# Convolution's input product: ten channel blocks with one product over both halves of x, and VectorE's order of taps and gates written out

## The chip, the cores and the metric

The kernel runs on one core of a Trainium2 chip. The metric is the time of one execution on the device in microseconds (us), the median of several runs. The engines are named as the profile names them: PE (matrix products), PEld (its weight loads), DVE (VectorE), ACT (ScalarE), POOL (GpSimd) and SP (which issues the weights' transfers).

## The reference

A decoder trunk of four residual layers over 256 tokens of 2048 channels, in float32: a convolution module, an MLP, a state-space layer, an MLP, and a last norm. The change lies in the convolution module, the first layer:

```python
def conv_module(h, w_in, b_in, dw, dw_b, ln_g, ln_b, w_out, b_out):
    u = h @ w_in + b_in                       # 256 x 2048 times 2048 x 4096
    a, gate = jnp.split(u, 2, axis=-1)
    v = a * jax.nn.sigmoid(gate)
    v = lax.conv_general_dilated(v, dw[:, None, :], ..., padding=[(30, 0)],
                                 feature_group_count=2048) + dw_b   # 31 taps per channel
    v = layer_norm(v, ln_g, ln_b)
    v = jax.nn.silu(v)
    return v @ w_out + b_out
```

## The kernel before, in words

**Products in float32.** Every operand is split into a high part (rounded to the fast matrix format) and a low part (what is left). A product is high x high + low x high + high x low. Activations lie as hT: channel blocks of 128 on the partitions, and for each block the high and the low part of the 256 tokens side by side (512 columns).

**The stream of weights.** Every layer adds its weights as *steps*; a step is 1 MB and is worked through in two *halves* of 0.5 MB. For each half, ACT converts the raw weights to the high part (L118, `hi`), and DVE or POOL subtracts to get the low part (L125, `lo`). In the convolution's input product the first eight halves have their low part made on DVE, halves 8 to 63 on POOL. There are four buffers each for `hi` and `lo`, so the conversion of a half waits until PE is through with the half four before. SP loads a step when the raw buffer of the step three before is free.

**The input product.** The 16 channel blocks c = 0..15 take four halves each (half h = 4c to 4c+3). Before, every block uses `mm_g`: per half 24 products of 256 columns (high weights with the high half of x, L211; high weights with the low half, L212; low weights with the high half, L213), all into one sum. The MLP's up product uses `mm_f` instead: eight products of 512 columns (high weights with both halves of x at once, L199), then eight of 256 (low weights, L202); the two sums lie side by side in the accumulator and have to be added later (`relu2`, L807 and L808).

**The gate of a block.** When a block's four halves are done, DVE multiplies the accumulator by the norm's factor (L446), ACT takes the sigmoid (L447, `ga`), and DVE combines both into the gated channel block (L448).

**Taps.** For c = 0..11 the depthwise convolution runs on DVE: ACT starts an accumulator (L527, `cv`), and 30 instructions on DVE add a tap each (L829). For c = 12..15 (`PACKED`) it runs on PE as 32 small products per block (L484, `pk`), from four shifted copies R. For 12 to 14 those copies go through DRAM: ACT's queue issues the write (L473, `vd`) and then the four reads (L477). For the last block, DVE and ACT copy them (L468, L470). The small weights for this, `wpk`, are made by ACT (16 small copies `dp`, L379) and POOL (L386). POOL also adds the output bias to x in four pieces (L398, L400).

**Layer norm.** After blocks 0..3 a first sum of their channels is made (L539, `stat`), copied by ACT (L558, `raw`), multiplied out (`mean`), and turned into a shift (L562). The groups 0..3, 4..7 and 8..11 have the shift taken off (L569, one instruction of DVE for four blocks), are squared on ACT (L571) and summed on PE (L539). After the last block the totals are made (`ln_totals`, `ln_finish`) and the output product begins.

**Order.** Each engine works through its own list in order. The lists are made when the program is built: a scheduler places the instructions by its own estimate of times, with `high_priority` for urgent ones, and `behind(x)` makes an instruction stand after x on its engine. The depthwise taps are emitted all 30 at once, so that the scheduler sets where they stand.

## Time and profile before

| | |
|---|---|
| median of 3 runs | 1988.23 us (1988.21 to 1988.59) |
| the profiled execution | 1987.61 us, span 1985.8 us |
| busy in the span | PE 99%, DVE 71%, ACT 48%, POOL 14% |
| granted PE clock | 1.00 in every slice |
| the convolution's input product | about 8 to 214 us of the span |
| PE idle or on small products after it, until the output product is under way | about 214 to 236 us |

The table is read with the profiled execution: it is 0.62 us below the median, and its span leaves out 1.8 us around it. Everything after 236 us is left as it is by the change, and each engine's list there is the same in both kernels.

### The profile page before, as it was taken

What the parts mean: (1) busy time and instruction counts of PE and PEld (TensorE: products, weight loads), DVE (VectorE), ACT (ScalarE), POOL (GpSimd) and SP (SyncE); (2) the same over time, 40 slices, a digit from 0 to 9 for tenths busy, and PEclk for the clock granted to TensorE, in tenths of its full rate; (3) what the DMA queues carried; (4) which work ended last, traced back from release to release, by engine and by line L of the source; (5) the groups of instructions that cost most, each with busy time, mean ns of one, the idle gap of its engine ahead of it and who ended that gap; (6) DMA issues with size and microseconds to landing.
All of it is one profiled execution on the core that took longest, in us unless ns stands there. A gap on an engine that the chain in (4) does not pass through costs nothing.

```text
span 1985.8 us, 28885 instructions
## 1 busy us (share of the span) xinstructions
PE 1966.9 (99%) x11604; PEld 1687.0 (85%) x11604; DVE 1401.3 (71%) x1904; ACT 952.4 (48%) x1179; POOL 274.8 (14%) x252
## 2 busy tenths in 40 slices
PE   8999999999999999999999999999999999999998
PEld 8999788888888888888888788888888888888887
DVE  6899798888787777777558847565555565555655
ACT  6443655544444544444445445454444454444444
POOL 3998300000000221222010000000000000000000
PEclk9999999999999999999999999999999999999999
DMA  8767458667686877877898865665666656565653
GB/s 228 190 184 207 147 183 267 206 226 245 200 260 192 214 229 253 265 246 238 319 308 298 304 215 186 191 191 189 193 190 192 190 191 191 190 213 190 192 191 128
DMA packets 317030, 428.49 MB, mean 216 GB/s; under 512 B 9761, under 2 KB 211553, under 8 KB 313537
## 3 DMA queue, kind: packets, MB, share of 16 engines
q1 hardware_dynamic: 300976, 384.59, 61.6%
q0 software_dynamic: 12352, 37.49, 6.3%
q10 hardware_dynamic: 3568, 4.56, 0.8%
q8 instruction: 91, 1.49, 0.3%
q14 instruction: 43, 0.35, 0.1%
HBM read 400.08 MB, written 34.91 MB: 219 GB/s over the span
## 4 chain that ended last, share of the span: by engine, by line
PE 96%; DVE 2%; DMA 1%; issue 0%; SPq 0%; POOL 0%; ACT 0%; POOLq 0%; DVEq 0%; ACTq 0%
PE acc L199 24%; PE acc L222 15%; PE acc L223 15%; PE acc L224 15%; PE acc L202 12%; PE acc L213 3%; PE acc L212 3%; PE acc L211 3%; PE pk L484 1%; DMA Vt<-Vd 0%; SPq L92 0%; PE kp L1113 0%; PE xw L1254 0%; DMA raw<-in_conv_w_in_dram 0%; PE xt L254 0%
## 5 line engine op out<-in xcount | busy, mean ns | idle before, releaser
L118 ACT ACTIVATE hi<-raw 128x1024 fp32r<-128x1024 f32 x672 | 711.6, 1060 | 953.5 <-PE acc L224 510.2
L125 DVE TENSOR_TENSOR lo<-raw,hi 128x1024 fp32r<-128x1024 f32 x611 | 747.9, 1226 | 505.6 <-ACT hi L118 501.3
L199 PE MATMUL acc<-hT,hi 128*128 128x512 f32 x2048 | 514.4, 393 | 0.0
L199 PEld LDWEIGHTS acc<-hT,hi 128*128 128x128 f32 x2048 | 368.9, 189 | 68.0 <-issue 1.6
L222 PE MATMUL acc<-hi,rT 128*128 128x512 f32 x992 | 387.2, 391 | 0.0
L223 PE MATMUL acc<-lo,rT 128*128 128x512 f32 x992 | 386.4, 390 | 0.0
L224 PE MATMUL acc<-hi,rT 128*128 128x512 f32 x992 | 386.0, 389 | 0.0
L202 PEld LDWEIGHTS acc<-hT,lo 128*128 128x128 f32 x2048 | 279.6, 190 | 20.0
L202 PE MATMUL acc<-hT,lo 128*128 128x256 f32 x2048 | 286.3, 282 | 0.0
L222 PEld LDWEIGHTS acc<-hi,rT 128*128 128x128 f32 x992 | 186.3, 188 | 39.6 <-issue 1.6
L224 PEld LDWEIGHTS acc<-hi,rT 128*128 128x128 f32 x992 | 186.3, 188 | 39.1
L223 PEld LDWEIGHTS acc<-lo,rT 128*128 128x128 f32 x992 | 186.3, 188 | 38.0 <-issue 0.2
L125 POOL TENSOR_TENSOR lo<-raw,hi 128x1024 fp32r<-128x1024 f32 x60 | 143.1, 2402 | 31.3 <-ACT hi L118 24.8
L211 PE MATMUL acc<-hT,hi 128*128 128x256 f32 x512 | 146.1, 286 | 0.9 <-ACT hi L118 0.9
L212 PE MATMUL acc<-hT,hi 128*128 128x256 f32 x512 | 145.7, 286 | 0.3 <-DVE hT L259 0.3
L213 PE MATMUL acc<-hT,lo 128*128 128x256 f32 x512 | 145.5, 286 | 0.0
L829 DVE SCALAR_TENSOR_TENSOR cv<-vT,dw,cv 128x256 f32<-128x256 f32 x348 | 141.3, 486 | 2.2 <-ACT cv L527 1.7
L820 DVE TENSOR_TENSOR x<-x,acc 128x1024 f32<-128x1024 f32 (+1 forms) x72 | 83.6, 1161 | 27.6 <-PE acc L224 22.0
L211 PEld LDWEIGHTS acc<-hT,hi 128*128 128x128 f32 x512 | 98.9, 193 | 3.0 <-issue 1.6
L222 PE MATMUL acc<-hi,yT 128*128 128x512 f32 x256 | 101.1, 395 | 0.0
L212 PEld LDWEIGHTS acc<-hT,hi 128*128 128x128 f32 x512 | 98.8, 193 | 2.2 <-issue 1.6
L223 PE MATMUL acc<-lo,yT 128*128 128x512 f32 x256 | 99.9, 390 | 0.6 <-DVE lo L125 0.6
(285 smaller groups left out, 1722.9 us busy)
## 6 DMA issues: line engine op xcount, KB each, us to landing
raw<-in_mlp_w_up_dram SPq DMA_DIRECT2D x128, 1024.0 KB, 5.8
raw<-in_mlp_w_down_dram SPq DMA_DIRECT2D x128, 1024.0 KB, 5.2
raw<-in_ssm_w_glu_dram SPq DMA_DIRECT2D x32, 1024.0 KB, 5.5
raw<-in_conv_w_in_dram SPq DMA_DIRECT2D x60, 512.0 KB, 5.6
...
```

Of the source, the lines that this page charges most:

```text
L118: self.nc.scalar.activation(hi, sl, AF.Copy)
L125: ins = eng.tensor_tensor(out=lo, in0=sl, in1=hi.bitcast(F32), op=ALU.subtract)
L199: mm(accs[m], lhsT=hi[:, kk, cs[m]], rhs=xT(k0 + kk), start=first and kk == 0, stop=False)
L202: mm(accs[m][:, 0:T], lhsT=lo[:, kk, cs[m]], rhs=xT(k0 + kk)[:, 0, :], start=False, stop=last and kk == 3)
L211: mm(accs[m], lhsT=hi[:, kk, c], rhs=x[:, 0, :], start=first and kk == 0, stop=False)
L212: mm(accs[m], lhsT=hi[:, kk, c], rhs=x[:, 1, :], start=False, stop=False)
L213: mm(accs[m], lhsT=lo[:, kk, c], rhs=x[:, 0, :], start=False, stop=last and kk == 3)
L222: mm(acc[:, b, :], lhsT=ak[:, 0, t], rhs=hi[:, kk, :], start=first and kk == 0, stop=False)
L223: mm(acc[:, b, :], lhsT=ak[:, 0, t], rhs=lo[:, kk, :], start=False, stop=False)
L224: self.mm_last = mm(acc[:, b, :], lhsT=ak[:, 1, t], rhs=hi[:, kk, :], start=False, stop=last and kk == 1)
L820: return self.nc.vector.tensor_tensor(out=out, in0=a, in1=b, op=op)
L829: return self.nc.vector.scalar_tensor_tensor(out=out, in0=a, scalar=s, in1=b, op0=op0, op1=op1)
```

## The change

1. For c = 3..12 (`HALVES`) the block uses `mm_f` in place of `mm_g`. The two sums are added in the gate: ACT copies the second one out of the accumulator (L457 of the changed kernel, `low`), and DVE adds it to the first (L458).
2. DVE's instructions of the stage (adds, multiplies, gates, taps, shifts) stand in one written order (`dve`). Taps are handed out in portions (`taps`): three between a block's multiply and its gate, then 3, 6, 7 and 6 with the next halves, which makes 25 per block, from two chains in turn. `begin_chains` starts an accumulator only when the number of open chains allows it.
3. On ACT, the next conversion of weights stands behind the sigmoid, or behind the `cv` that was started last (`act_first`).
4. In the norm, the group is summed when its last tap is done, the shift stands two halves later, and the centring of a group is emitted at once.

```diff
+HALVES = range(3, 13)
...
-            self.nc.scalar.activation(hi, sl, AF.Copy)
+            with self.behind(self.act_first) if self.act_first is not None else nullcontext():
+                self.nc.scalar.activation(hi, sl, AF.Copy)
+            self.act_first = None
...
-                    self.mm_g([A[:, 0], A[:, 1]], self.hT, hi, lo, kc * 8 + half * 4,
-                              kc == 0 and half == 0, kc == 1 and half == 1)
+                    (self.mm_f if c in HALVES else self.mm_g)([A[:, 0], A[:, 1]], self.hT, hi, lo, kc * 8 + half * 4,
+                                                              kc == 0 and half == 0, kc == 1 and half == 1)
                     if kc == 1 and half == 1:
-                        self.gate(c, A)
+                        self.gate(c, acc)
+                    h = 4 * c + 2 * kc + half
+                    if h >= 6 and not (c == KB - 1 and kc == 1 and half == 1):
+                        self.taps(3 if kc == 1 and half == 1 else 7 if half else 6)
...
-            nc.vector.tensor_tensor(out=A, in0=A, in1=self.rstdB.broadcast_to([P, 2, T]), op=ALU.mult)
-            nc.scalar.activation(t, A[:, 1, :], AF.Sigmoid, bias=b_in[:, KB + c:KB + c + 1])
-            nc.vector.scalar_tensor_tensor(out=self.cblk(c), in0=A[:, 0, :], scalar=b_in[:, c:c + 1], in1=t,
-                                           op0=ALU.add, op1=ALU.mult)
+            if c in HALVES:
+                low = self.t2([P, 2, T], name="low")
+                nc.scalar.activation(low, acc[:, :, T:2 * T], AF.Copy)
+                self.dve(lambda: nc.vector.tensor_tensor(out=A, in0=A, in1=low, op=ALU.add))
+            self.dve(lambda: nc.vector.tensor_tensor(out=A, in0=A, in1=self.rstdB.broadcast_to([P, 2, T]), op=ALU.mult))
+            self.act_first = nc.scalar.activation(t, A[:, 1, :], AF.Sigmoid, bias=b_in[:, KB + c:KB + c + 1])
+        self.taps(3)
+        with self.tc.high_priority(offset=URGENT):
+            self.dve(lambda: nc.vector.scalar_tensor_tensor(out=self.cblk(c), in0=A[:, 0, :], scalar=b_in[:, c:c + 1], in1=t,
+                                                            op0=ALU.add, op1=ALU.mult))
...
+    def dve(self, fn):
+        with self.behind(self.dv) if self.dv is not None else nullcontext():
+            self.dv = fn()
+
+    def begin_chains(self):
+        while self.waiting and len(self.chains) < (2 if any(x[0] == EARLY - 1 for x in self.chains) else 3):
+            c = self.waiting.pop(0)
+            acc = self.bank([P, T], name="cv")
+            self.act_first = self.nc.scalar.activation(acc, self.vb(c)[:, 0:T], AF.Identity, scale=self.dw[:, c, 0:1],
+                                                       bias=self.vec("dw_b")[:, c:c + 1])
+            self.chains.append([c, acc, 1])
+
+    def taps(self, n):
+        for _ in range(n):
+            if not self.chains:
+                return
+            self.turn = (self.turn + 1) % min(2, len(self.chains))
+            x = self.chains[self.turn]
+            c, acc, j = x
+            last = j == TAPS - 1
+            self.dve(lambda: self.stt(self.cblk(c) if last else acc, self.vb(c)[:, j:j + T], self.dw[:, c, j:j + 1], acc,
+                                      ALU.mult, ALU.add))
+            x[2] += 1
+            if last:
+                self.chains.remove(x)
+                self.ln_feed(c)
+                self.begin_chains()
...
-            self.after(2, self.ln_shift)
+            self.after(1, self.ln_shift)
         else:
-            self.after(2, lambda: self.centre(g[0], 4))
+            self.centre(g[0], len(g))
...
+        def use():
+            self.dve(lambda: nc.vector.tensor_scalar(out=self.shift, in0=ps, scalar1=1.0 / (EARLY * P), scalar2=None,
+                                                     op0=ALU.mult))
+            self.centre(0, EARLY)
+        self.after(2, use)
```

Three places of the engines' lists are shown here; a row is a line of the code, the operation, and tile<-tiles, with xN for N in a row. The first is ACT's list at the start of the stage, before: the conversions of halves 6 to 9, the table load and the sigmoid of block 0, its `cv`, the 16 small copies.

```order
L118 ACTIVATE hi<-raw 128x1024 x4
L447 ACT_TABLE_LOAD
L447 ACTIVATE ga<-acc,vecs 128x256
L527 ACTIVATE cv<-vT,vecs,dw 128x256
L379 ACTIVATE dp<-dw 32x4x8 x16
```

In the changed kernel the same place, from half 6's conversion on:

```order
L120 ACTIVATE hi<-raw 128x1024
L460 ACT_TABLE_LOAD
L460 ACTIVATE ga<-acc,vecs 128x256
L481 ACTIVATE cv<-vT,vecs,dw 128x256
L120 ACTIVATE hi<-raw 128x1024 x4
```

and further down the same list, from half 15's conversion to half 22's:

```order
L120 ACTIVATE hi<-raw 128x1024 x4
L457 ACTIVATE low<-acc 128x512
L382 ACTIVATE dp<-dw 32x4x8 x16
L460 ACTIVATE ga<-acc,vecs 128x256
L481 ACTIVATE cv<-vT,vecs,dw 128x256
L120 ACTIVATE hi<-raw 128x1024 x4
```

The conversions of halves 7 to 9 moved behind block 0's sigmoid and `cv`, and the 16 small copies moved from there to between block 3's `low` and its sigmoid, with half 19's conversion behind them.

POOL's list behind half 19's low part, before (an L386 row makes one block's `wpk`, an L398 row fetches a piece of the output bias, an L400 row adds a piece to x):

```order
L386 TENSOR_TENSOR wpk<-dp,m_244 128x1024
L125 TENSOR_TENSOR lo<-raw,hi 128x1024 x8
L386 TENSOR_TENSOR wpk<-dp,m_244 128x1024
L125 TENSOR_TENSOR lo<-raw,hi 128x1024 x4
L398 DMA bo<-in_conv_b_out_dram 128x512
L125 TENSOR_TENSOR lo<-raw,hi 128x1024
L398 DMA bo<-in_conv_b_out_dram 128x512
L125 TENSOR_TENSOR lo<-raw,hi 128x1024
L400 TENSOR_TENSOR x<-x,bo 128x2x512
```

and now:

```order
L389 TENSOR_TENSOR wpk<-dp,m_244 128x1024
L128 TENSOR_TENSOR lo<-raw,hi 128x1024 x3
L401 DMA bo<-in_conv_b_out_dram 128x512
L128 TENSOR_TENSOR lo<-raw,hi 128x1024 x3
L403 TENSOR_TENSOR x<-x,bo 128x2x512
L128 TENSOR_TENSOR lo<-raw,hi 128x1024 x2
L389 TENSOR_TENSOR wpk<-dp,m_244 128x1024
L128 TENSOR_TENSOR lo<-raw,hi 128x1024 x3
L401 DMA bo<-in_conv_b_out_dram 128x512
L403 TENSOR_TENSOR x<-x,bo 128x2x512
L128 TENSOR_TENSOR lo<-raw,hi 128x1024 x5
```

The pieces of bias moved to earlier halves, and the second piece's addition now stands right behind its transfer.

The second place is the first centring. On DVE, before, from block 6's gate on (taps, the shift, the centring of blocks 0 to 3):

```order
L448 SCALAR_TENSOR_TENSOR vT<-acc,vecs,ga 128x256
L829 SCALAR_TENSOR_TENSOR cv<-vT,dw,cv 128x256 x6
L562 TENSOR_SCALAR shift<-mean 128x256
L829 SCALAR_TENSOR_TENSOR cv<-vT,dw,cv 128x256 x2
L569 TENSOR_TENSOR vT<-vT,shift 128x4x256
```

and in the changed kernel, from block 6's add on:

```order
L458 TENSOR_TENSOR acc<-acc,low 128x2x256
L459 TENSOR_TENSOR acc<-acc,bcs 128x2x256
L869 SCALAR_TENSOR_TENSOR cv<-vT,dw,cv 128x256 x3
L463 SCALAR_TENSOR_TENSOR vT<-acc,vecs,ga 128x256
L869 SCALAR_TENSOR_TENSOR cv<-vT,dw,cv 128x256 x9
L600 TENSOR_SCALAR shift<-mean 128x256
L608 TENSOR_TENSOR vT<-vT,shift 128x4x256
```

On PE, in the changed kernel, from the low products of half 26 to the sums of the centred blocks (a row of L202 holds a half's eight high products, a row of L205 its eight low ones; behind the first row they are of halves 28, 27, 28, 29, 29, 30, 30):

```order
L205 MATMUL acc<-hT,lo 128x256 x8
L202 MATMUL acc<-hT,hi 128x512 x8
L205 MATMUL acc<-hT,lo 128x256 x8
L575 MATMUL stat<-vT,ones 32x256
L205 MATMUL acc<-hT,lo 128x256 x8
L202 MATMUL acc<-hT,hi 128x512 x8
L596 MATMUL mean<-raw,q_246 128x256
L205 MATMUL acc<-hT,lo 128x256 x8
L202 MATMUL acc<-hT,hi 128x512 x8
L205 MATMUL acc<-hT,lo 128x256 x8
L575 MATMUL stat<-vT,ones 32x256 x4
```

Before, the shift and the centring stood six and eight taps behind block 6's gate on DVE, and PE's first sum of centred blocks stood ten products into half 31; now nine taps stand ahead of both, and PE's sum stands at the end of half 30.

The third place is ACT's list from block 12's sigmoid on, before (the conversions are of halves 56 to 58; an L473 row is the write to DRAM, an L477 row a read back):

```order
L447 ACTIVATE ga<-acc,vecs 128x256
L118 ACTIVATE hi<-raw 128x1024
L473 DMA vd_2335<-vT 128x288
L118 ACTIVATE hi<-raw 128x1024
L477 DMA R<-vd_2335 32x4x284 x3
L118 ACTIVATE hi<-raw 128x1024
L477 DMA R<-vd_2335 32x4x284
L527 ACTIVATE cv<-vT,vecs,dw 128x256
```

and now (the conversions are of half 55, and of halves 56 to 58):

```order
L460 ACTIVATE ga<-acc,vecs 128x256
L120 ACTIVATE hi<-raw 128x1024
L520 DMA vd_1956<-vT 128x288
L524 DMA R<-vd_1956 32x4x284 x4
L481 ACTIVATE cv<-vT,vecs,dw 128x256
L120 ACTIVATE hi<-raw 128x1024 x3
```

Half 56's conversion moved from ahead of the write to behind the four reads, which wait for the write. At the end of the stage, on DVE, the last taps of blocks 10 and 11 and the centring of blocks 8 to 11 (L569) stood ahead of block 15's multiply; now three taps stand between block 15's multiply and its gate, and block 11's last tap and the centring stand behind the eight copies of R.

32 lines of the change are left out of this document (13 added, 19 removed).

## The prediction

> **What bounds the kernel now.** I read the page first: busy time by engine, then the chain that ended last.
>
> ```profile
> PE 1966.9 (99%) x11604; PEld 1687.0 (85%) x11604; DVE 1401.3 (71%) x1904; ACT 952.4 (48%) x1179; POOL 274.8 (14%) x252
> PE 96%; DVE 2%; DMA 1%; issue 0%; SPq 0%; POOL 0%; ACT 0%; POOLq 0%; DVEq 0%; ACTq 0%
> ```
>
> PE sets the time, and whatever shifts PE in the changed stage shifts the end: behind 236 us every list is as it was. The same holds inside the stage. In windows cut at the starts of channel blocks (PE alone: length, busy time, records, clock) PE is never idle. The rows are blocks 3, 4, 7, 9, 14 and 15.
>
> ```profile
> 50.20:61.72 11.52, 11.52 (x98) 1.00 0.82 219
> 61.72:73.97 12.25, 12.25 (x100) 1.00 0.66 179
> 98.48:112.65 14.17, 14.17 (x118) 1.00 0.80 220
> 124.17:135.99 11.82, 11.78 (x99) 1.00 0.51 135
> 182.19:198.99 16.80, 16.80 (x178) 1.00 0.83 225
> 198.99:214.30 15.31, 15.31 (x162) 1.00 0.71 221
> ```
>
> A plain block takes 11.52 us, a half 11.52/4 = 2.88, one 256-column product 2.88/24 = 0.120. What goes beyond 11.52 is PE's other work (sums for the norm; packed taps in the last two), and in block 9 one wait of about 0.3 for POOL, seen in the chain:
>
> ```profile
> 131.04 2.42 POOL lo L125
> 133.50 0.39 PE acc L213
> ```
>
> I count 0.4 us of such waits; they are gained if POOL is no worse later.
>
> **The saving.** The MLP runs the new form already. The chain there reads, for one half:
>
> ```profile
> 366.64 1.84 PE acc L199 x8
> 368.48 0.95 PE acc L202 x8
> ```
>
> 1.84 + 0.95 = 2.79 a half against 2.88; 40 halves x 0.09 = **-3.6**. With the 0.4 above, 4.0 us is all that the change can win. The Trainium skill ("TensorE: Matmul & The Clock Gate", the section with the back-to-back gaps) gives columns / 2.4 GHz plus about 2.5 ns per product; by that, a pair of 256 columns costs 2.6 ns more than one of 512, an estimated 0.8 us over 320 pairs. The rows say 2 x 120 against 230 ns, and the rows decide.
>
> **What it adds.** The copies and adds of the two sums have their like in `relu2`:
>
> ```profile
> L807 ACT ACTIVATE t<-acc x64: 576/586/602, 340.0 to 1890.7; 128x512 f32<-128x512 f32 x64
> L808 DVE TENSOR_TENSOR t<-acc,t x64: 677/684/687, 341.2 to 1892.0; 128x512 f32<-128x512 f32 x64
> ```
>
> Ten of each, 5.9 us on ACT and 6.8 on DVE, cost nothing by themselves; they hide under PE's next block. But they lengthen what follows, and the conversions now stand behind it. I walk each place, and set an engine's chain against the products that PE still has in hand (`hi` and `lo` have four buffers).
>
> *Half 7 (start).* Now `hi` of half 7 stands behind block 0's sigmoid and `cv`.
>
> ```profile
> 26.69 1.06 ACT L118 ACTIVATE hi<-raw 128x1024 fp32r<-128x1024 f32 x1 [0.52 <-PE acc L212]
> 29.34 1.22 DVE L125 TENSOR_TENSOR lo<-raw,hi 128x1024 fp32r<-128x1024 f32 x1
> 32.39 1.11 PE dwt L353 x16
> 34.89 0.66 DVE L355 COPY dw<-dwt 128x496 f32<-128x496 f32 x1
> 35.65 0.57 ACT L527 ACTIVATE cv<-vT,vecs,dw 128x256 f32<-128x256 f32 x1 [1.19 <-DVE dw L355]
> ```
>
> The `dwt` products end at 33.5, the copy at 34.2, `cv` at 34.8, `hi` at 35.9, DVE's `lo` at 37.1. PE starts half 7 at 50.20 - 11.52 - 2.88 = 35.8 and wants its low part four products of 0.12 later, near 36.3. **+0.9**.
>
> *Halves 19 and 20 (the small copies).* The 16 copies now stand between block 3's `low` and its sigmoid.
>
> ```profile
> 36.16 4.28 ACT L379 ACTIVATE dp<-dw 32x32 f32<-32x32 f32 x16
> 65.36 1.92 POOL L386 TENSOR_TENSOR wpk<-dp,m 128x1024 f32<-128x1024 f32 x1
> 154.20 26.04 POOL L125 TENSOR_TENSOR lo<-raw,hi 128x1024 fp32r<-128x1024 f32 x11
> ```
>
> From block 3's last product: low 0.6, copies 4.3, sigmoid 0.5, `cv` 0.6, `hi` 1.1, handing over 0.6: 7.7 us to half 19's `hi`. PE has half 16's low products, 17 and 18: 0.95 + 2 x 2.79 = 6.55. Wait 1.1. Then POOL makes `lo` 19, `wpk`, `lo` 20: 2.37 + 1.9 + 2.37 = 6.7, while PE has 1.84 + 0.95 + 1.84 = 4.6. Wait 2.05. Together **+3.1**. Before, the copies ran at 36.16, and POOL was 5.7 us ahead: it was through with `lo` 19 when `wpk` began at 65.36, and PE came to half 19 at 61.72 + 12.25 - 2.88 = 71.1. Of the price, 1.1 is gone if `dp` is cut short, 2.05 if POOL comes with a lead; both at once cost nothing, and with a slower hand-over the place costs up to 4.
>
> *Halves 28 to 31 (first centring).*
>
> ```profile
> 53.78 0.48 DVE L448 SCALAR_TENSOR_TENSOR vT<-acc,vecs,ga 128x256 f32<-128x256 f32 x1
> 54.18 8.71 DVE L829 SCALAR_TENSOR_TENSOR cv<-vT,dw,cv 128x256 f32<-128x256 f32 x22
> 62.79 0.69 DVE L446 TENSOR_TENSOR acc<-acc,bcs 128x512 f32<-128x512 f32 x1
> 100.67 0.39 ACT L558 ACTIVATE raw<-stat 128x256 f32<-128x256 f32 x1 [0.62 <-PE stat L539]
> L569 DVE TENSOR_TENSOR vT<-vT,shift x3: 1683/1737/2411, 105.2 to 210.6; 128x1024 f32<-128x1024 f32 x3
> ```
>
> A tap takes (62.79 - 54.18)/22 = 0.39, a gate 0.40 to the next start. From block 6's last product: the sum of block 3 0.73 (block 4's 12.25 - 11.52), `raw` 0.4, low 0.6, add 0.7, multiply 0.6, three taps 1.2, gate 0.4, nine taps 3.5, shift 0.35, centring 1.7: 10.2. PE has that sum, three low parts, two high ones and `mean` (0.4, an estimate: about half a sum): 7.7. Wait 2.5; the sum of block 3 itself waits some 0.3 for its last tap, which stands two taps ahead of the add. **+2.8**. Before, the shift stood six taps behind the gate, and PE's sum ten products into half 31, so nothing waited. If DVE were quicker, POOL is late next. From `lo` 20 to `lo` 48 it has 28 x 2.37, three `wpk`, three additions and three transfers of bias (0.6 each to issue):
>
> ```profile
> 151.84 2.39 POOL L400 TENSOR_TENSOR x<-x,bo 128x1024 f32<-128x1024 f32 x1
> DMA to landing us min/median/max: 3.4/4.0/5.0
> ```
>
> The second addition stands right behind its transfer (the landing is `bo`'s), so POOL also sits out 3.4: 66.4 + 5.7 + 7.2 + 1.8 + 3.4 = 84.5. PE has 28 x 2.79 = 78.1 and the sums, 0.73 x 3 + (14.17 - 11.52) = 4.8: 82.9. POOL alone would make it wait 1.6, inside the 2.8.
>
> *Half 56 (block 12's copies through DRAM).* Before, ACT did this for block 13:
>
> ```profile
> 185.49 0.35 ACTq L473 DMA_DIRECT2D vd<-vT  x1
> 190.26 1.85 ACTq L477 DMA_DIRECT2D R<-vd  x3
> 192.22 1.06 ACT L118 ACTIVATE hi<-raw 128x1024 fp32r<-128x1024 f32 x1 [4.45 <-issue]
> DMA to landing us min/median/max: 1.7/4.2/4.8
> ```
>
> The reads wait in ACT's list until the write has landed (the last row is `vd`'s), and the next conversion waits behind them, 4.45 us. Now half 56's conversion stands there. The Trainium skill ("DMA: Bandwidth & Descriptors", anatomy of one DMA) says so too: a wait is held on the issuing sequencer, before dispatch. Its formula, 2.0 us plus bytes over 436 GB/s, would give the 144 KB write an estimated 2.3 us and the sum 1 us less. I take 3.3, the middle of 1.7 and 4.8. DVE comes late as well: per block 25 x 0.39 + add 0.6 + multiply 0.6 + gate 0.4 = 11.4 against PE's 11.17, and 1.7 for the second centring; over blocks 9 to 12 that is 47.3, against PE's 44.7. Lag 2.6, if DVE starts that stretch on time. From block 12's last product: lag 2.6 (the low copy is done by then), add 0.7, multiply 0.6, taps 1.2, gate 0.4, write 0.35 and 3.3, four reads 1.8, `cv` 0.6, `hi` 1.1, `lo` 2.4, handing over 0.2: 15.3. PE has block 13's 11.5. **+3.8** (2.2 to 5.3 by the landing; about nothing with no lag and the short landing). Blocks 13 and 14 have a conversion between write and reads as before, and DVE is less late there, since only half of its work is left: nothing.
>
> *At nothing.* The second centring's sum stands behind half 48 on PE, three halves after DVE is asked for it; its 1.7 us is in DVE's lag. SP's loads are issued when a raw buffer comes free, and the DMA engines are busy 0.51 to 0.83 in the rows of the blocks, so they keep up with a stage that gets longer.
>
> *One pair of sums* (block 12 and its square) moves from the tail to before block 15's end: **+0.65**, a little under block 4's 0.73, since part of it runs between packed products.
>
> *Tail.*
>
> ```profile
> 210.63 1.74 DVE L569 TENSOR_TENSOR vT<-vT,shift 128x1024 f32<-128x1024 f32 x1
> 212.40 1.06 ACT L571 ACTIVATE sq<-vT 128x1024 f32<-128x1024 f32 x1 [3.58 <-DVE vT L569]
> 214.49 0.70 DVE L446 TENSOR_TENSOR acc<-acc,bcs 128x512 f32<-128x512 f32 x1 [1.73 <-PE acc L213]
> 216.41 3.89 DVE L470 COPY R<-vT 32x284 f32<-32x284 f32 x8
> 225.01 0.48 DVE L829 SCALAR_TENSOR_TENSOR vT<-pk,vecs,shift 128x256 f32<-128x256 f32 x1 [0.41 <-PE pk L484]
> ```
>
> Before, 225.01 - 214.49 = 10.5 us from block 15's multiply to its last step, the centring of blocks 8 to 11 being done. Now: multiply 0.6, three taps 1.2, gate 0.4, copies 3.9, tap 0.4, block 14's step 0.4, centring 1.7, square 1.1, then PE's sums ahead of the last packed products, some 2, handing over 1.1: 12.8. The ends are 0, if the sums lose nothing on PE's own packed products, and 3.5, if each hand-over is as long as the 0.7 ahead of block 15's gate before. **+2.3**.
>
> **Sum.** -3.6 - 0.4 + 0.9 + 3.1 + 2.8 + 3.8 + 0.65 + 2.3 = +9.5. The profiled execution took 1987.61 us (span 1985.8), so 1997.1; it lies 0.62 below the median of 1988.23, so **1997.7** on the scale of the median.
>
> **Rivals.**
>
> *The new form gives slack.* It frees a half's `hi` 0.95 us sooner, after its high products, and wants its `lo` only 1.84 us into the half. I have counted this once, in PE's work at each place; if the chains profit from it on both sides (a conversion starts sooner and is wanted later), each of the four waits gains up to 2.8, and of 0.9, 3.1, 2.8 and 3.8 little is left. With a tail as before that is 1988.2 - 4.0 = 1984.2, faster. It decides where waits and tail come to less than 0.1. For it speaks that the MLP's stage runs this form without a wait; against it, that there ACT and POOL have no `dp`, no bias and no reads in their lists: 7.7 against 6.55 and 84.5 against 82.9 need no lag. Chance 0.10.
>
> *Half hidden.* No lag on DVE and a landing of 1.7 leave half 56 without a wait (-3.8), and the tail ends as before (-2.3): +3.4, 1991.6. Chance 0.22.
>
> *DVE becomes the bound.* With 11.4 against 11.17 it has no spare in these blocks. If a tap takes 0.42 from two chains in turn, four blocks bring 25 x 0.03 x 4 = 3 us more of lag ahead of `vd`: 2000.7 and above. For it: DVE has 22 taps between two gates before, and 25 now. Against it: nothing in the rows makes a tap longer. Chance 0.10.
>
> *The saving isn't there.* If a high product of 512 columns takes 237 ns here, 3 ns under a pair, 0.9 is left of 3.6: 2000.4. Against it, the 230 holds for all eight products of the row above. That is also about what the gaps of the Trainium skill's page on TensorE would make of the change; by the rows of this trace they don't hold here. Chance 0.08.
>
> **How the numbers follow.** My forecast has 0.50. A change of 0.2% (4.0 us), about what a measurement can tell from none, parts the cases: slower 0.50 + 0.10 + 0.08 = 0.68; within it, half hidden, 0.22; faster 0.10. The forecast's own range is 1993.5 to 2001.5 (half 56's two ends, the tail's, the copies' 4). To leave out no more than 2 in 10 I reach into half hidden and past DVE's case: 1986 to 2002.5.
>
> **What would show it.** In the changed profile: L202 at 0.23 and L205 at 0.12 from start to start in ten blocks; PE waiting for DVE's `lo` near 36 us, for `hi` and POOL's `lo` near 71 to 78, for DVE's centring (a sum at L575) near 112, for POOL's `lo` near 187 to 191, with ACT idle behind the reads; block 15's multiply near 221.7 instead of 214.49, its last step 12.8 us later. I am wrong if PE stays busy through 70 to 80 us, if the write lands under 2 us, or if that last step follows in 10.5.

## The result, and the profile after

| | before | changed |
|---|---|---|
| median (6 runs each) | 1988.41 us (1987.42 to 1989.26) | 2005.59 us (2002.55 to 2007.54) |
| ratio, with its 95% interval | | 1.0084 (1.0071 to 1.0097) |
| the profiled execution, its span | 1987.61, 1985.8 us | 2005.66, 2003.9 us |

The changed kernel is slower, by 17.2 us where 9.5 were forecast. In the traces the output product starts 16.88 us later; the 1.2 us that the spans differ beyond that appear at about 1085 us, where PE runs at half clock once more in this execution and not in that of before. First the page of the changed kernel: busy time, and the chain that ended last.

```profile
PE 1971.3 (98%) x11284; PEld 1673.0 (83%) x11284; DVE 1411.5 (70%) x1914; ACT 954.7 (48%) x1189; POOL 275.8 (14%) x252
...
PE 91%; DVE 5%; issue 1%; DMA 1%; POOL 1%; ACT 0%; SPq 0%; POOLq 0%; DVEq 0%; ACTq 0%
```

DVE's share of the chain went from 2% to 5%, and PE's busy time rose by 4.4 us although its products became fewer. Next, the waits of PE from 20 to 260 us (waited for; us in total, times, longest):

```profile
PE stat L575 <- DVE vT L608: 5.4, 2, 4.1
PE acc L216 <- POOL lo L128: 2.4, 3, 1.9
PE pk L531 <- DVE R L516: 2.4, 2, 2.2
PE acc L205 <- POOL lo L128: 1.8, 1, 1.8
PE acc L202 <- ACT hi L120: 0.9, 1, 0.9
PE acc L214 <- ACT hi L120: 0.8, 2, 0.4
```

These waits are 13.7 us in all. They stand at the places that the prediction names and at two that it put at nothing or left open: a second wait for the centring (L608), and one for the copies R in the tail. The rise in busy time is in the windows of PE alone (length, busy time and records, granted clock; the last two columns are of the DMA engines). The first pair begins at half 20, the others at the first centring, half 56 and the tail:

```profile
74.47:77.88 3.41, 1.81 (x12) 1.00 0.80 221
77.88:81.29 3.41, 3.19 (x19) 1.00 0.35 87
112.02:115.43 3.41, 0.98 (x10) 1.00 0.00 0
115.43:118.84 3.41, 3.41 (x10) 0.50 0.21 48
...
190.53:193.94 3.41, 1.65 (x12) 1.00 1.08 242
193.94:197.35 3.41, 2.86 (x13) 0.50 0.91 177
...
231.49:234.90 3.41, 1.22 (x6) 1.00 0.33 70
234.90:238.31 3.41, 3.25 (x33) 0.50 0.69 259
```

Behind three of the waits PE works at half clock, for 3.41 us each. The kernel before has 1.00 throughout from 20 to 260 us. The prediction has no term for this.

The windows are cut where the clock changes, and they show what decides. The half-clock stretches of a trace lie on one grid: those of this trace start at 115.43, 193.94, 234.90 and 1084.82 us, which are 23, 12 and 249 times 3.413 us apart, and apart from the last microseconds of a trace each lasts one, two or four such windows in every run here. What counts is how long PE was idle within one window: 2.43, 1.76 and 2.19 us in the three that are followed by half clock. Of the 1.82 us at half 20, 1.60 fell into one window and the rest into the next, and the clock stayed at 1.00. Over all windows at full clock in the twenty traces (from 20 us on, without the last 5), half clock followed each of the 28 with 1.9 us or more of idle time, none with less than 1.74, and 7 of the 13 between. Where the grid lies differs from trace to trace, so whether a wait of about 1.8 us brings the half clock is chance.

The timeline shows the first two centrings of the changed kernel with what stands around them (start, duration, engine, line; in brackets the idle time ahead, and what ended it):

```profile
110.97 2.33 POOL L403 TENSOR_TENSOR x<-x,bo 128x1024 f32<-128x1024 f32 x1 [3.97 <-DMA bo<-in_conv_b_out_dram]
111.05 3.34 DVE L608 TENSOR_TENSOR vT<-vT,shift 128x1024 f32<-128x1024 f32 x1
111.05 0.57 ACT L481 ACTIVATE cv<-vT,vecs,dw 128x256 f32<-128x256 f32 x1 [4.94 <-DVE shift L600]
114.44 0.64 PE L575 MATMUL stat<-vT,ones 128*32 128x256 f32 x8 [4.12 <-DVE vT L608]
...
165.72 2.39 POOL L403 TENSOR_TENSOR x<-x,bo 128x1024 f32<-128x1024 f32 x1
165.78 3.42 DVE L608 TENSOR_TENSOR vT<-vT,shift 128x1024 f32<-128x1024 f32 x1
169.25 0.64 PE L575 MATMUL stat<-vT,ones 128*32 128x256 f32 x8 [1.27 <-DVE vT L608]
```

and its source view gives all three (shortest, median, longest in ns):

```profile
L608 DVE TENSOR_TENSOR vT<-vT,shift x3: 1217/3343/3419, 111.0 to 235.9; 128x1024 f32<-128x1024 f32 x3
```

The third ran while POOL was idle and took 1.22 us. The first two took 3.3 and 3.4. Both end 1.09 us after POOL's addition of the bias ends: 110.97 + 2.33 + 1.09 = 114.39, and 165.72 + 2.39 + 1.09 = 169.20. The three of the kernel before obey the same sum:

```profile
103.37 2.39 POOL L125 TENSOR_TENSOR lo<-raw,hi 128x1024 fp32r<-128x1024 f32 x1 [0.66 <-ACT hi L118]
105.17 1.68 DVE L569 TENSOR_TENSOR vT<-vT,shift 128x1024 f32<-128x1024 f32 x1
...
177.84 2.40 POOL L125 TENSOR_TENSOR lo<-raw,hi 128x1024 fp32r<-128x1024 f32 x1
178.91 2.41 DVE L569 TENSOR_TENSOR vT<-vT,shift 128x1024 f32<-128x1024 f32 x1
```

105.76 + 1.09 = 106.85; 180.24 + 1.09 = 181.33; and, by the row at 210.63 in the prediction, 212.37 where POOL ended at 211.28. So the 1.68, 1.74 and 2.41 us that the prediction used were a 1.2 us instruction held up by what POOL happened to be doing.

To see where delay arises in each kernel, I take the start of a half's last product and subtract the same time of the kernel before. "out" is the first output product. All the kernels below are in the table; they are told in the next section. (Single readings carry up to 2 us of other order: the next half's high products can stand ahead of a half's low ones, and the second group's sums, 1.4 us, stand at half 56 before and at 48 to 49 in the changed kernel.)

```
half              7     20     30     34     47     55     58     63    out
changed        0.85   2.30   1.89   7.34   7.47   9.33  13.06  13.44  16.88
order_only     0.90   0.26   0.26   1.49   1.56  10.79  10.93  10.46  14.13
halves_only   -0.47  -1.21  11.99  10.14   8.34  16.72  14.98  17.33  17.89
order_psum     1.21   0.57   0.58   2.28   4.70   5.56   5.99   5.52   8.91
psum           0.89   2.34   1.50   4.29   6.53   7.94  11.38  12.22  15.35
sum_late       0.93   2.37   1.54   4.28   5.83  12.72  15.26  15.64  19.78
psum_late      0.70   2.15   1.32   6.16   6.84   8.22  13.48  14.31  17.43
warm_fill      0.98   2.44   3.15  13.46  12.66  20.72  24.41  23.94  28.72
warm_fill2     1.37   2.80   1.97   8.53   7.68  14.67  18.00  17.53  20.58
all5           0.83  -0.97  -0.30   6.52   7.51   8.15   9.03   9.87  10.06
after_nofirst -0.36  -1.87  -3.87   0.84   4.37   8.37   6.89   8.49  11.06
all6          -0.36  -2.16  -2.34  -2.28   2.55   5.09   3.35   4.18   5.30
all7          -0.51  -2.02  -4.02   2.19   3.31   7.65   6.14   8.23  13.79
all6_order     0.03  -0.94  -0.70  -1.02  -1.63  -0.21  -1.95  -1.12  -0.92
all8           0.29  -1.51  -1.75  -1.33   0.10   2.82   8.25   6.81   7.00
all8_lock      0.04  -1.75  -2.00  -2.67  -0.33   3.68   7.45   6.01   6.07
all6_h5       -0.05  -1.85  -2.04  -0.74   1.08   3.56   1.82   2.66   5.94
all8_h5       -0.43  -2.22  -2.47  -1.51  -0.44   2.03   1.91   1.45   1.65
after_bias     0.95   2.39   1.16  10.56  10.55  11.73  20.14  18.28  20.96
```

Where nothing waits, the delay of the changed kernel falls by 0.09 us a half (7.51, 7.42, 7.34 at halves 32 to 34): the saving of the product form is there, as large as forecast.

### The profile page after: what moved, and what is told of

The parts are those of the page before. It is cut to its first block, busy times and chain, and to the rows that moved or that the text cites. A ratio compares the mean times of both kernels' runs of the same rounds, so it can differ in the third digit from the quotient of the medians.

```text
span 2003.9 us, 28244 instructions
## 1 busy us (share of the span) xinstructions
PE 1971.3 (98%) x11284; PEld 1673.0 (83%) x11284; DVE 1411.5 (70%) x1914; ACT 954.7 (48%) x1189; POOL 275.8 (14%) x252
## 4 chain that ended last, share of the span: by engine, by line
PE 91%; DVE 5%; issue 1%; DMA 1%; POOL 1%; ACT 0%; SPq 0%; POOLq 0%; DVEq 0%; ACTq 0%
PE acc L202 24%; PE acc L225 15%; PE acc L226 15%; PE acc L227 15%; PE acc L205 13%; DVE cv L869 2%; PE acc L214 1%; PE acc L216 1%; PE acc L215 1%; POOL lo L128 1%; PE pk L531 1%; DMA raw<-in_conv_w_in_dram 1%; PE xt L257 1%; PE kp L1153 0%; DMA Vt<-Vd 0%
## 5 line engine op out<-in xcount | busy, mean ns | idle before, releaser
L202 PE MATMUL acc<-hT,hi 128*128 128x512 f32 x2368 | 595.4, 394 | 0.9 <-ACT hi L120 0.9
L202 PEld LDWEIGHTS acc<-hT,hi 128*128 128x128 f32 x2368 | 427.9, 189 | 81.4 <-issue 2.8
L205 PEld LDWEIGHTS acc<-hT,lo 128*128 128x128 f32 x2368 | 322.2, 190 | 26.1 <-POOL lo L128 2.0
L205 PE MATMUL acc<-hT,lo 128*128 128x256 f32 x2368 | 331.2, 283 | 1.8 <-POOL lo L128 1.8
L225 PE MATMUL acc<-hi,yT 128*128 128x512 f32 x256 | 101.1, 395 | 0.0
L227 PE MATMUL acc<-hi,yT 128*128 128x512 f32 x256 | 99.7, 390 | 0.0
L216 PE MATMUL acc<-hT,lo 128*128 128x256 f32 x192 | 56.0, 294 | 2.4 <-POOL lo L128 2.4
L214 PE MATMUL acc<-hT,hi 128*128 128x256 f32 x192 | 56.2, 294 | 1.7 <-ACT hi L120 1.7
L225 PEld LDWEIGHTS acc<-hi,yT 128*128 128x128 f32 x256 | 48.1, 188 | 10.9 <-issue 1.0
```

The source lines that it names most:

```text
L202: mm(accs[m], lhsT=hi[:, kk, cs[m]], rhs=xT(k0 + kk), start=first and kk == 0, stop=False)
L205: mm(accs[m][:, 0:T], lhsT=lo[:, kk, cs[m]], rhs=xT(k0 + kk)[:, 0, :], start=False, stop=last and kk == 3)
L214: mm(accs[m], lhsT=hi[:, kk, c], rhs=x[:, 0, :], start=first and kk == 0, stop=False)
L216: mm(accs[m], lhsT=lo[:, kk, c], rhs=x[:, 0, :], start=False, stop=last and kk == 3)
L225: mm(acc[:, b, :], lhsT=ak[:, 0, t], rhs=hi[:, kk, :], start=first and kk == 0, stop=False)
L227: self.mm_last = mm(acc[:, b, :], lhsT=ak[:, 1, t], rhs=hi[:, kk, :], start=False, stop=last and kk == 1)
```

## The experiments

Every edit is on the changed kernel unless said. Times are medians; the ratio is against the kernel before on the same chip.

**One part alone.** `order_only` keeps the order and drops the product form; `halves_only` puts the product form, its copy and its add into the kernel before and leaves the order to the scheduler.

```diff
 order_only:
-HALVES = range(3, 13)
+HALVES = ()
 halves_only (on the kernel before):
+            if c in HALVES:
+                low = self.t2([P, 2, T], name="low")
+                nc.scalar.activation(low, acc[:, :, T:2 * T], AF.Copy)
+                nc.vector.tensor_tensor(out=A, in0=A, in1=low, op=ALU.add)
```

> The kernel before, with the one product over both halves of x in blocks 3 to 12 and the two sums added in the gate; the order of everything is left to the scheduler as before. Theory A (the written order and what it does to ACT's, POOL's and DVE's lists costs the time, the product form saves its 3.6 us): 1984 to 1987 us, PE without a wait over 2 us in the stage. Theory B (the product form itself costs it: PE runs ahead of POOL and DVE, and the add lengthens the gate): 1995 us or more, with PE waiting for POOL's low parts or DVE's centring.

> The changed kernel with no block in the new product form: no copies and adds of a second sum, all else as changed (the written order of VectorE, the conversions behind the sigmoid, the sums and centring of the norm). Theory A: the places that wait are still there, a little smaller because PE has 0.36 us more work in a block and DVE no add: 1996 to 2004 us. Theory B: near the kernel before, within 4 us.

`order_only`: 2001.47 us, ratio 1.0069 (1.0054 to 1.0084). `halves_only`: 2005.10, 1.0089 (1.0074 to 1.0104). Each part alone costs nearly as much as both, so the parts do not add; each runs into waits of its own. In `order_only` the second centring lasts 8.5 us, and PE waits for it:

```profile
155.78 9.36 POOL L128 TENSOR_TENSOR lo<-raw,hi 128x1024 fp32r<-128x1024 f32 x4
157.71 8.52 DVE L608 TENSOR_TENSOR vT<-vT,shift 128x1024 f32<-128x1024 f32 x1
```

```profile
PE stat L575 <- DVE vT L608: 5.2, 1, 5.2
```

155.78 + 9.36 + 1.09 = 166.23 = 157.71 + 8.52: the centring waited out the POOL instruction that it met and the three behind it. `halves_only` shows it once more, behind three low parts (175.12 + 7.00 + 1.09 = 183.21):

```profile
173.34 9.87 DVE L576 TENSOR_TENSOR vT<-vT,shift 128x1024 f32<-128x1024 f32 x1
...
175.12 7.00 POOL L126 TENSOR_TENSOR lo<-raw,hi 128x1024 fp32r<-128x1024 f32 x3
```

```profile
PE stat L546 <- DVE vT L576: 7.2, 2, 4.9
PE stat L546 <- DVE vT L836: 6.7, 3, 5.0
```

There PE also meets its sums before the taps are done (L836), since the scheduler places them by its estimate; these waits, 13.9 us together, and half clock for 13.65 and 6.83 us behind them make up its 17 us.

**The lock-out.** The centring reads two operands from SBUF. In `order_psum` and `psum` it reads one of them from PSUM instead: blocks 0 to 3 subtract the mean straight from the sums' bank, blocks 4 to 11 subtract the shift from the taps' accumulator ahead of the last tap.

```diff
+            for c in range(EARLY):
+                self.dve(lambda: self.stt(self.cblk(c), ps, -1.0 / (EARLY * P), self.cblk(c), ALU.mult, ALU.add))
...
+            if last and c >= EARLY:
+                self.dve(lambda: self.stt(acc, acc, 1.0, self.shift, ALU.mult, ALU.subtract))
...
-        self.dve(lambda: nc.vector.tensor_tensor(out=v, in0=v, in1=self.shift.unsqueeze(1).broadcast_to([P, n, T]),
-                                                 op=ALU.subtract))
```

> The changed kernel with no block in the new product form (as in order_only), and the centring no longer one instruction with two operands in SBUF: blocks 0 to 3 take four instructions that read the mean straight from PSUM, blocks 4 to 11 take the shift off their sum in PSUM just ahead of the last tap. In order_only the second centring lasted 8.5 us beside POOL's low parts and cost PE 9.2 us with the half clock. Theory C (VectorE's instruction with two SBUF operands is shut out as long as POOL runs without a pause; with an operand in PSUM it is not): every piece of the centring lasts 0.4 to 0.5 us whatever POOL does, PE's wait there is gone, 1991 to 1995 us. Theory D (the centring is slow because of what runs at that time, memory or transfers, whichever operands it has): pieces of 1 us and more, 1999 to 2003 us.

> The changed kernel with the centring from PSUM as in order_psum, the new product form in blocks 3 to 12 as changed. Theory C: pieces of 0.4 to 0.5 us; PE's first wait shrinks from 4.1 us to 2.3 (four pieces take 1.6 instead of 3.3), the second, 1.3, goes: 2000 to 2003.5 us. Theory D: pieces of 0.8 us or more and no gain, 2004.5 to 2007 us.

`order_psum` (with `HALVES = ()`): 1996.47 us, 1.0049 (1.0034 to 1.0064), 5.0 below `order_only`. `psum`: 2004.66, 1.0086 (1.0071 to 1.0101), only 0.9 below the changed kernel. By form, DVE's groups of `order_psum` (count, busy us, mean ns):

```profile
L871 DVE SCALAR_TENSOR_TENSOR cv<-cv,shift 128x256 f32<-128x256 f32 x8 | 3.4, 424 | 0.0
...
L871 DVE SCALAR_TENSOR_TENSOR vT<-mean,vT 128x256 f32<-128x256 f32 x4 | 1.4, 418 | 0.0
```

Twelve pieces of 0.42 us in place of three instructions of up to 8.5, and the wait of 5.2 is gone. Seven of the pieces ran while a POOL instruction was running, and none of them is longer for it. So the long centring came from its two operands in SBUF together with POOL. The edit also made the pieces shorter, and no short piece with both operands in SBUF was run; but being short does not keep an instruction clear by itself: of the tail's eight copies of R from SBUF to SBUF, most of which take 0.30 us, one ends 0.16 us after a low part of POOL in 18 of the twenty traces, and takes 1.69 to 2.37 us (2.18 in the changed kernel). In `psum` the wait at half 31 also shrinks (the delay at half 34 falls from 7.34 to 4.29), but conversions are late next, so little is won at the end:

```profile
PE acc L202 <- ACT hi L120: 2.7, 3, 1.0
```

The Trainium skill ("SBUF — State Buffer", the section on SBUF's two separate sides) says that GpSimd and a VectorE instruction with two SBUF inputs share one port pair under an exclusive lock, which the one that starts first holds for its whole instruction. The traces agree on the lock, also in the other direction: POOL's instruction behind a centring that got in lasts 3.37 us in place of 2.37. They differ in that VectorE, already waiting, was kept out by up to three further POOL instructions.

**PE's sums later.** `sum_late` asks for the sums of the first two centred groups three halves later and puts them behind low products; `psum_late` is `psum` with four. In PE's list this moves the first group's sums from behind half 30 to behind half 31 and half 32; the second group's stay behind half 48.

```diff
+        def sums():
+            with self.behind(self.mm_last):
                 self.colsum(self.stat[:, 0, :], cs, lambda i: self.cblk(cs[i]), True)
                 self.colsum(self.stat[:, 1, :], cs, lambda i: sq[:, i, :], False)
+        self.after(LATE, sums)
```

> The changed kernel with PE's first sums of the centred blocks one half later in PE's list: behind the low products of half 31 instead of those of half 30. Theory A (the wait of 4.1 us for the centring, and the 1.7 us at half clock behind it, come from where the sums stand): the wait is gone or under 1 us, 4 to 6 us less than the changed kernel, 1999.5 to 2001.5. Theory B (POOL is late next: its list allows PE no more): PE waits for POOL's low part of half 31 instead, 2 to 3 us less than the changed kernel.

> As psum, and PE's sums of the centred blocks of the first two groups stand four halves later in PE's list than they are asked for. Theory A and C together: neither group makes PE wait, no stretch at half clock before half 56: 7 to 9 us less than the changed kernel at half 48, 1997 to 2000 us in all. Rival (POOL is late next, since the waits hid how far it lags): PE waits for POOL's low parts of halves 28 to 40 instead, 2002 us or more.

`sum_late`: 2006.31 us, 1.0089 (1.0074 to 1.0104); `psum_late`: 2006.38, 1.0096 (1.0081 to 1.0111). Nothing is won. In `sum_late` the first wait became one of 2.3 us for ACT's `hi`, and the delay at half 34 fell from 7.34 to 4.28; but the second centring met the end of a low part and had to wait out the three POOL instructions behind it:

```profile
163.64 8.35 DVE L609 TENSOR_TENSOR vT<-vT,shift 128x1024 f32<-128x1024 f32 x1
163.91 2.40 POOL L404 TENSOR_TENSOR x<-x,bo 128x1024 f32<-128x1024 f32 x1
166.28 4.63 POOL L128 TENSOR_TENSOR lo<-raw,hi 128x1024 fp32r<-128x1024 f32 x2
```

166.28 + 4.63 + 1.09 = 172.00 = 163.64 + 8.35. In `psum_late` PE waits for ACT's `hi` in the sums' place, 3.6 us: the wait for the centring had covered most of it.

**The clock.** `warm_fill` and `warm_fill2` put small products into PE's three waits (at the first centring, half 56 and the tail), to keep the clock up.

```diff
+    def fill(self, n, ps, ins):
+        with self.behind(ins):
+            for _ in range(n):
+                ins = self.nc.tensor.matmul(ps, lhsT=self.ident, rhs=self.ident, start=True, stop=True, ...)
+        return ins
```

> The changed kernel with small products on PE, whose result nobody reads, in three places where PE sat idle: 30 ahead of the first sums of the centred blocks, 16 ahead of half 56, 16 ahead of block 15's packed taps. Theory A (an idle PE is granted half its clock for some 3.2 us afterwards, and each such stretch costs 1.4 to 1.7 us): no slice under 1.00 in these places, and 3 to 5 us less than the changed kernel, 2000.5 to 2002.5. Theory B (PE waits there for the other engines anyway, so that the clock costs nothing): within 1 us of the changed kernel.

> As warm_fill, with fewer of the small products, since one of them took 0.23 us there and not half of that, so that 30 of them held PE up by themselves: 13 ahead of the first sums of the centred blocks, 8 ahead of half 56, 8 ahead of block 15's packed taps. Theory A (an idle PE is granted half its clock for some 3.2 us afterwards): no half clock behind the first sums, and PE 1.4 to 1.7 us less late at the end of half 34 than in the changed kernel (7.3 us there); in all 2 to 5 us less unless the second centring meets a longer run of POOL. Theory B (the clock costs nothing, PE waits there anyway): half 34 as late as in the changed kernel, within 0.3 us.

`warm_fill` (30, 16, 16 products): 2016.26 us, 1.0140 (1.0123 to 1.0157); `warm_fill2` (13, 8, 8): 2009.48, 1.0109 (1.0092 to 1.0125). A filling product takes 0.24 us, twice what I had planned, so `warm_fill` held PE up by itself. It also shows the grid at work: half 20 waits for POOL's low part for 1.81 us there, as in the changed kernel (1.82), but here the wait fell into a single window, and half clock from 79.10 us followed. `warm_fill2` fits, and holds the clock at the first centring, half 56 and the tail. Its high products of two halves behind the first centring, and those of the changed kernel:

```profile
115.95 3.96 PE L209 MATMUL acc<-hT,hi 128*128 128x512 f32 x16 [1.07 <-ACT hi L120]
```

```profile
115.02 5.53 PE L202 MATMUL acc<-hT,hi 128*128 128x512 f32 x16
```

One half-clock stretch costs 5.53 - 3.96 = 1.57 us. But here too something else was late next (ACT's `hi`, 1.07), so that 0.6 us were left of it (at half 33, where both kernels have the same order, the delay is 6.80 in place of 7.42; the 8.53 at half 34 is a reading of another order). And the second centring came 0.28 us sooner against POOL than in the changed kernel: 0.22 ahead of the bias addition, in place of 0.06 behind it. It then lasted 8.31 us:

```profile
165.51 8.31 DVE L624 TENSOR_TENSOR vT<-vT,shift 128x1024 f32<-128x1024 f32 x1
165.73 2.42 POOL L411 TENSOR_TENSOR x<-x,bo 128x1024 f32<-128x1024 f32 x1
168.09 4.64 POOL L128 TENSOR_TENSOR lo<-raw,hi 128x1024 fp32r<-128x1024 f32 x2
```

So centrings a quarter of a microsecond apart took 3.4 and 8.3 us. That the changed kernel's runs spread over 5 us (2002.55 to 2007.54) would fit this, and would as well fit the place of the clock's grid; I saw the trace of one of them only.

**The lists, step by step.** `all5` adds to `psum_late` the small copies `dp` seven halves earlier, the four reads R one half later, and lets DVE make all taps that are left from half 61 on. `all6` further lets conversions go ahead of `cv`, `all7` ahead of the sigmoid too. `after_nofirst` does only these last two to the changed kernel. `all6_order` is `all6` without the product form.

```diff
 all5 (on psum_late):
-        self.after(16, prep)
+        self.after(9, prep)
-            self.after(1, fetch)
+            self.after(2, fetch)
-                        self.taps(3 if kc == 1 and half == 1 else 7 if half else 6)
+                        self.taps(TAPS * KB if h >= 61 else 3 if kc == 1 and half == 1 else 7 if half else 6)
 all6:
-            self.act_first = self.nc.scalar.activation(acc, self.vb(c)[:, 0:T], ...)
+            self.nc.scalar.activation(acc, self.vb(c)[:, 0:T], ...)
 all7 (and after_nofirst, with the edit of all6):
-            self.act_first = nc.scalar.activation(t, A[:, 1, :], AF.Sigmoid, ...)
+            nc.scalar.activation(t, A[:, 1, :], AF.Sigmoid, ...)
```

> As psum_late, and three more: the 16 small copies of ACT are asked for seven halves earlier, the reads from DRAM one half later, and VectorE hands out all taps that are left from half 61 on. Theory: each place of the prediction's sum that waited is gone, so that the product form's 3.6 us show up: 1984 to 1988 us, with PE's longest wait in the stage under 1 us. Rival (VectorE has no spare in these blocks, so its lag comes out in block 12 and in the tail whatever the order): 1990 to 1996 us, with a wait ahead of half 56 and after block 15.

> As all5, but a conversion no longer stands behind a started accumulator, only behind the sigmoid. In all5 the start of block 6's accumulator waited 6.3 us on ACT for the PSUM bank that the mean held, four conversions behind it, and PE waited 5.8 us for half 31. Theory E: that wait and its half clock go, 7 us less than all5: 1990 to 1994 us. Rival (POOL's low parts or VectorE's taps are late next in the same place): 1995 us or more, with PE waiting there for another engine.

> As all6, and no conversion stands behind the sigmoid either; ACT's order is the scheduler's. Theory E: the wait of half 7 goes too, 0.9 us less than all6. Rival (without the rule the scheduler puts a conversion ahead of a sigmoid that VectorE needs, and its lag grows): 2 us or more above all6.

> The changed kernel without the rule that a conversion of weights stands behind the sigmoid or the last started accumulator; ACT's order is the scheduler's again, all else as changed. Theory E (part of the loss is ACT's list: conversions queued behind an accumulator that waits for a free PSUM bank, and behind the 16 small copies): the waits of halves 7 and 19 go, about 3 us of the 17, while the two centrings keep theirs: 2000 to 2004 us. Rival (these waits lie beside VectorE's and change nothing): 2004.5 us or more.

> As all6, with no block in the new product form. Theory F (with the waits gone the product form is worth what its products save, 40 halves by 0.09 us): 3 to 4 us above all6. Rival (PE is 3.6 us earlier and then waits for VectorE or POOL, so that nothing of it arrives): within 1 us of all6, or below it.

| | us | ratio (95%) |
|---|---|---|
| all5 | 2000.33 | 1.0067 (1.0050 to 1.0084) |
| all6 | 1993.73 | 1.0033 (1.0021 to 1.0046) |
| all7 | 2001.62 | 1.0068 (1.0055 to 1.0080) |
| after_nofirst | 1998.12 | 1.0054 (1.0038 to 1.0069) |
| all6_order | 1987.30 (before 1987.39) | 1.0001 (0.9993 to 1.0010) |

`all5` ends 6 us below `psum_late`: half 20 waits 0.4 us in place of 0.9 and 1.8 at halves 19 and 20, half 56 waits 1.9 in place of 2.6 and 1.6, without the half clock behind, and the tail costs 0.2 us in place of 3.1 (63 to out). The longest wait that is left stands in one row. `cv` waits for its PSUM bank until the mean in it has been read, and four conversions stand behind `cv`:

```profile
112.37 0.57 ACT L483 ACTIVATE cv<-vT,vecs,dw 128x256 f32<-128x256 f32 x1 [6.26 <-DVE vT L877]
112.88 3.88 ACT L121 ACTIVATE hi<-raw 128x1024 fp32r<-128x1024 f32 x4
113.97 5.31 PE L203 MATMUL acc<-hT,hi 128*128 128x512 f32 x16 [5.84 <-ACT hi L121]
```

`all6` takes that queue away and is 6.6 us faster. `all7` loses it again. With conversions free to go ahead of the sigmoid, DVE's gate comes late, and PE waits for the accumulator that the gate frees (5.7 us), as in `after_nofirst`, which is still 7.5 us below the changed kernel:

```profile
PE acc L202 <- DVE vT L463: 7.9, 5, 2.1
```

So tying the conversions to the sigmoid is worth 7.9 us (`all7` against `all6`), and tying them to `cv` costs. `all6_order` equals the kernel before, and PE has no long wait left until the output product; the longest group is

```profile
PE acc L229 <- DVE sT L243: 0.6, 2, 0.3
```

All that the written order cost is thereby found: two operands from SBUF, the place of PE's sums, of `dp`, of the reads, of the last taps, and the queue behind `cv`. (The parts were added together, so their single shares are known only as far as the rows above go.)

**What takes the saving.** `all6` against `all6_order` is the product form alone, with these waits mended: it should give -3.6 and gives +6.4. `all8` moves the four bias additions on POOL behind half 52; `all8_lock` is `all8` with the centring from SBUF again; `after_bias` does only the bias move to the changed kernel; `all6_h5` and `all8_h5` use the form in blocks 3 to 7 only.

```diff
 all8, all8_lock, after_bias:
-            self.after(20 + 8 * i, lambda i=i: self.add_b_out(i))
+            self.after(50 + 4 * i, lambda i=i: self.add_b_out(i))
 all6_h5, all8_h5:
-HALVES = range(3, 13)
+HALVES = range(3, 8)
```

> As all6, with the four additions of the output bias moved from halves 20 to 48 of POOL's list to halves 52 and later. In all6 PE was 2.3 us ahead of the kernel before at half 34 and then waited 5.2 us for POOL's low parts. Theory G (with VectorE's and ACT's waits gone, POOL's list is what the faster products run into; its bias additions and transfers are the part too much): PE has no wait over 0.5 us for POOL, 1983 to 1986.5 us. Rival H (VectorE's 11.4 us a block against 11.17 of PE makes it late by block 12 whatever POOL does): a wait for VectorE's gate or for half 56 instead, 1987.5 to 1991 us.

> As all8, with the centring as one instruction with two operands in SBUF again, as in the changed kernel. Theory C (it is shut out while POOL runs without a pause): a centring of several us, as long as POOL's run goes on plus 1.1 us; VectorE comes that much later to the next block, 2 to 8 us above all8. Rival (PE's sums stand late enough now, and VectorE catches up): within 1 us of all8.

> The changed kernel with only the four bias additions moved behind half 51. POOL then runs low parts without a pause where the centrings stand. Theory C and G: the first centring, which got in behind an addition after 3.3 us, now waits for POOL's whole run; if POOL has no pause there, PE loses more than the 2 to 4 us that POOL's shorter list gives: 2004 to 2010 us. Rival (POOL's lag is what counts): 1998 to 2003 us.

> As all6, with the new product form in blocks 3 to 7 alone. Theory H (in these blocks VectorE and POOL have less time for their work on a block than it takes, so their lag grows with each block in the new form; five such blocks, and then blocks in which PE takes 11.52 us, let them catch up): PE about 1.8 us ahead at half 34 and still so at half 55, 1984.5 to 1987 us, 0.5 to 2.5 us below all6_order. Rival (the form costs its share in each block, whichever follow): halfway between all6 and all6_order, 1989 to 1991.5 us.

> As all6_h5, with the bias additions moved behind half 51 as in all8. Theory G and H together: POOL has no lag either, at most 0.5 us below all6_h5: 1984 to 1987 us. Rival (additions late in the stage make POOL late for the packed blocks): 1 us or more above all6_h5.

| | us | ratio (95%) |
|---|---|---|
| all8 | 1996.39 | 1.0043 (1.0030 to 1.0055) |
| all8_lock | 1995.41 | 1.0036 (1.0023 to 1.0050) |
| after_bias | 2009.78 | 1.0113 (1.0098 to 1.0129) |
| all6_h5 | 1994.36 | 1.0032 (1.0020 to 1.0044) |
| all8_h5 | 1990.56 | 1.0014 (1.0005 to 1.0023) |

In `all6` PE leads the kernel before by 2.3 us until half 34, and then waits for POOL's low parts; in `all8` PE waits 1.9 us for POOL in place of 5.2, but the copies R of block 12 come late. DVE's gate of that block stands 5.6 us later than in `all6_order`, and the write and the reads take some 3 us longer to land:

```profile
PE acc L206 <- POOL lo L129: 5.2, 4, 2.3
```

```profile
PE pk L535 <- DMA R<-vd: 2.1, 1, 2.1
```

So `all8` came out above both times that were expected of it. Five blocks cost as much as ten (`all6_h5` against `all6`), which neither of the expectations has: 3.3 us of it arise behind half 63, where PE waits 2.3 us for a step of DVE that stands behind the eight copies, and goes on at half clock. With five blocks and the bias late (`all8_h5`) +2.9 us are left, and no kernel with the form reached the one before. I read this so: neither engine alone takes the saving. A half of 2.79 us leaves POOL (2.37 a half, with `wpk`, bias and their transfers) and DVE (11.4 us a block by the prediction's count) without room to catch up, and a wait of 2 us can bring the half clock with it. No run shows this by itself, and how the loss divides between the two in ten blocks stays open. `all8_lock` equals `all8` within the intervals, against the expectation: its first two centrings took 1.95 and 2.29 us, each let in behind the POOL instruction that it met, although POOL had four low parts in a row there. `after_bias` was meant to show this on the changed kernel and does not, though its time lies in the range that was expected: its three centrings do take 1.22 us each, with POOL idle, but the scheduler moved block 3's sum and the mean down in PE's list, to right ahead of the sums of the centred blocks (the mean from 105.99 to 109.43 us). ACT's `raw` waits for the one, block 6's `low` stands behind `raw`, and DVE's add comes 5.2 us later. So PE waits longer than before:

```profile
PE stat L575 <- DVE vT L608: 7.5, 1, 7.5
```

## Why the prediction was wrong

The changed kernel is 17.2 us slower, outside the range of 1986 to 2002.5 us. The direction, its cause (waits at named places cost more than 3.6 us of shorter products), and most of the places were right. By its terms:

| term | forecast | in the trace |
|---|---|---|
| product form, 40 halves | -3.6 | -0.09 a half, as forecast |
| half 7 | +0.9 | +1.2 |
| halves 19 and 20 | +3.1 | 0.91 + 1.82 = +2.7 |
| first centring | +2.8 | 0.35 + 4.12 idle and 1.57 of half clock = +6.0 |
| second centring | 0 | +1.3 |
| half 56 | +3.8 | 0.26 + 0.36 + 1.94 idle, and 1.4 of half clock = +4.0 |
| one pair of sums | +0.65 | +0.8 |
| tail | +2.3 | 16.88 - 13.44 = +3.4 |

With the 0.4 of old waits these come to 15.4; the other 1.5 of 16.88 are small steps that I do not assign.

**The failed step is the first centring, with the second.** The prediction priced the centring at 1.7 us from three rows that read 1683, 1737 and 2411 ns. The runs showed 1.22 us with POOL idle, and 3.34 and 3.42 us at the two places that count, where POOL's bias addition had begun 0.08 and 0.06 us earlier: waits of 4.12 and 1.27 us in place of 2.5 and none. The same instruction on the same tile should not vary by 0.7 us; the rows themselves, set beside POOL's, gave the sum "POOL's end + 1.09" before any run. That POOL would start just there was not to be foreseen; that a price of 1.7 us was not safe, was. The second centring was costed at nothing because its sum stands "three halves after DVE is asked for it". DVE came to it only at 165.78 us, PE to the sum at 167.98: 1.7 us would still have fitted, 3.42 did not.

**No term for the clock.** The prediction puts nothing behind the waits that it adds. The profile before shows 1.00 through the stage, where PE idles at most 0.4 us at a time. A forecast that adds waits of 2 to 4 us to PE must ask what follows them. Here each of three was followed by 3.41 us at half clock, about 1.4 to 1.6 us each: 4 to 5 of the 7.7 us that were missing (the tail's share is within its +3.4). The Trainium skill ("TensorE: Matmul & The Clock Gate", Part 1) has a clock of either full or half rate and an idle window of about 3.4 us; the traces agree on the two rates and on the length, 3.41 us. They differ in that PE need not be idle for a whole window: 1.76 us within one were enough here.

**Half 56 was right only in its sum, by luck.** The write landed in 1.94 us where 3.3 were taken, and under 2 us is one of the signs of being wrong that the prediction names. DVE began block 12's add 3.9 us after that block's last product where 2.6 were taken. PE waited 2.57 us in all, and the half clock added 1.4. The prediction's estimate of 2.3 us was nearer. (The formula behind it, from the Trainium skill ("DMA: Bandwidth & Descriptors", anatomy of one DMA), is fitted there on transfers that GpSimd issues; this write is ACT's.)

**The tail** was short by 1.1. From block 15's multiply to its last step:

```profile
227.93 0.70 DVE L459 TENSOR_TENSOR acc<-acc,bcs 128x512 f32<-128x512 f32 x1 [2.52 <-PE acc L216]
...
230.16 2.35 POOL L128 TENSOR_TENSOR lo<-raw,hi 128x1024 fp32r<-128x1024 f32 x1 [6.28 <-ACT hi L120]
230.50 4.57 DVE L516 COPY R<-vT 32x284 f32<-32x284 f32 x8
233.68 1.28 PE L531 MATMUL pk<-R,wpk 128*32 128x256 f32 x6 [2.19 <-DVE R L516]
...
242.07 0.48 DVE L869 SCALAR_TENSOR_TENSOR vT<-pk,vecs,shift 128x256 f32<-128x256 f32 x1
```

14.1 us against 12.8. The eight copies took 4.57 us in place of 3.89: the first of them, which met POOL's low part nearer to its start than before, took 2.18 us in place of 1.69. PE idled 2.19 us on them, and went on at half clock. The work left for the tail was the larger part: in `all5`, where DVE makes all taps from half 61 on, and the centring's pieces with them, the tail costs 0.2 us with copies just as long (4.76).

**The rivals.** *The new form gives slack* is refuted in its mechanism: in `all6`, where without the form no long wait is left, the form loses 6.4 us rather than winning. *DVE becomes the bound* names a pressure that is there (in `after_nofirst` PE waits five times for the gate), though a tap stayed at 0.39 us and did not become 0.42. *Half hidden* and *the saving isn't there* did not happen: the tail and half 56 cost what is in the table, and the 0.09 a half is in the trace.
